# Two tile pairs by seven products beside one plain pair, in a two-block transformer kernel on one Trainium2 core

## The chip, the core and the metric

The kernel runs on one core of a Trainium2 chip. The core's engines are PE (TensorE, the matrix multiplier), DVE (VectorE), ACT (ScalarE), POOL (GpSimd) and SP (SyncE, which here issues the loads of the weights). Each runs its own instruction stream and waits for the others on semaphores. The metric is the device time of one execution in microseconds (us).

## The reference

A hidden state of 1024 features by 528 positions (16 learned ones and 512 of the input) goes through an attention layer, a gated feed-forward network (FFN), a latent-attention layer, a second FFN, and a mixing layer with a third FFN. All is float32. The change lies in the three FFNs, which compute

```
xn = rms_norm(h, g_norm)
a, b = jnp.split(xn @ w_in, 2, axis=-1)          # 2 x 2816 columns
ap = jnp.pad(a, ((0, 0), (CONV_W - 1, 0), (0, 0)))
a_conv = conv_b
for j in range(CONV_W):                          # causal, width 3
    a_conv = a_conv + ap[:, j:j + L] * conv_w[j]
return h + (jax.nn.silu(a_conv) * b) @ w_out
```

2816 columns are 22 tiles of 128, so `w_in` has 22 tile pairs: tile f of the half a, and tile 22 + f of the half b.

## The kernel before, in words

**Products.** The state lies with features on the 128 partitions (8 tiles, k = 0 to 7) and positions along the free axis. Each float32 operand is split in a high and a low part, and each product is three matmuls: high weights by high state (`Xh`), high by low (`Xl`), low by high. A weight tile of 128 outputs by 1024 features is thus 24 matmuls over some columns.

**A plain tile pair** (`plain`, L553) takes 96 matmuls of about half the columns: two pieces of tile a, two of tile b. In the second FFN tile b, and in the third both tiles, go in one piece of 512 columns (24 matmuls) in place of two of 256. Each result goes through DVE and ACT (`gate`: convolution, SiLU) to the tile `G`, input of `w_out`.

**A tile pair by seven products** (`pair`, L565) is Winograd's form of a 2 by 2 block product: the blocks are the two tiles by two halves of the features, against two halves of the features by two halves of the positions (H = 264, 258 or 256 columns). Seven block products of 12 matmuls each (84 in all) replace eight. They need sums of weight blocks and differences of state blocks. With a1 and a2 the two weight tiles of a pair, four weight sets are made in turn, and I name them by the `kind` in the plan of weights: "a" (a1 itself, products p1 and p2), "s" (a2's first half plus its second, and that less a1's first half: p5 and p6), "t" (two more differences, written over a1: p7 and p3), "d" (a2's second half: p4). The differences of the state (`T`, as `Th` and `Tl`) are made once in an FFN by `differences` (L489 to L509), behind the first plain pair. Each seven is interleaved with one plain pair, and PE keeps that order as written (`in_order`); the other engines' orders are set by a scheduler.

**Weights** (`Weights`, L79 to L173). A plan lists the weight tiles in the order of their use. Loads of 512 KB run three entries ahead on SP (L101), into a pool of three raw buffers; the second row a2 of a seven has one buffer of its own, "rawA". The split in high and low runs two entries ahead: ACT casts the high part (L147, `whi`), DVE subtracts the low part (L154, `wlo`), or POOL does (L151) for kind "d" and for plain tiles with n % 4 == 3. There are four buffers for split weights, and one more ("ws") for kind "s". POOL makes the sums (L110): those of kind "s" in one buffer "rawS", those of kind "t" over a1. The differences of the state are also made in the buffer "rawS" (L497).

**The FFN** runs its 22 tile pairs in three groups (`GROUPS`, L59). In each, `group_h` then multiplies the group's part of `G` by `w_out` (matmuls into `po`).

Of the kernel before, what the change touches and what calls it, by code (L numbers as in the profile page):

```python
# [12 lines left out]
F32 = mybir.dt.float32  # L13
# [8 lines left out]
P = 128  # L22
D = 1024
KD = D // P
META = 16
# [15 lines left out]
def _layout_params():  # L41
# [15 lines left out]
NPAR = _layout_params()  # L57

GROUPS = (  # L59
# [3 lines left out]
)  # L63

WSPEC = [
# [13 lines left out]
class Weights:  # L79
# [7 lines left out]
    def __init__(self, net, plan, gains, raw, parts, load_ahead, split_ahead):  # L87
        self.net, self.plan, self.gains = net, plan, gains
        self.raw, self.parts = raw, parts
        self.la, self.sa = load_ahead, split_ahead  # L90
        self.nl = self.ns = self.nu = 0
        self.raws, self.split = {}, {}
        self.more = None

    def load(self):
        key, aps, nk, nc_, kind = self.plan[self.nl]
        ts = []
        for i, ap in enumerate(aps):
            pool, tag, kw = (self.more, "rawA", {"bufs": 1}) if i else (self.raw, "raw", {})
            t = pool.tile([P, 1024], F32, tag=tag, name=f"raw{self.nl}_{i}", **kw)  # L100
            self.net.nc.sync.dma_start(t[:, : ap.shape[-1]], ap)  # L101
            ts.append(t)
        if ts:
            self.raws[self.nl] = ts
        self.nl += 1

    def sums(self, d, a, b, op):
# [4 lines left out]
    def source(self, n, kind, w):  # L112

        lo, hi = slice(0, 512), slice(512, 1024)
        if kind == "":
            return self.raws.pop(n)[0][:, :w]
        if kind == "a":
            self.A = self.raws.pop(n)
            return self.A[0]
        a1, a2 = self.A  # L120
        if kind == "s":
            self.S = self.more.tile([P, 1056], F32, tag="rawS", name=f"rawS{n}", bufs=1)
            self.sums(self.S[:, lo], a2[:, lo], a2[:, hi], ALU.add)
            self.sums(self.S[:, hi], self.S[:, lo], a1[:, lo], ALU.subtract)
            return self.S[:, :1024]
        if kind == "t":
            self.sums(a1[:, lo], a1[:, lo], a2[:, lo], ALU.subtract)
            self.sums(a1[:, hi], a1[:, hi], self.S[:, hi], ALU.subtract)
            return a1
        return a2[:, hi]  # L130

    def _split(self):
        nc = self.net.nc
# [53 lines left out]
class Net:  # L187
# [60 lines left out]
    def plan_ffn(self, wi, wo):  # L248
        pl = []
        for k0, k1, steps in GROUPS:  # L250
            for st in steps:
                if isinstance(st, int):
                    pl += [self.chunk(wi, st), self.chunk(wi, NF + st)]
                    continue
                f, g = st
                rows = [self.chunk(wi, m)[1][0] for m in (f, NF + f)]
                pl += [((wi, f, "a"), rows, 8, P, "a"), ((wi, f, "s"), [], 8, P, "s"), self.chunk(wi, g)]
                pl += [((wi, f, "t"), [], 8, P, "t"), self.chunk(wi, NF + g), ((wi, f, "d"), [], 4, P, "d")]
            pl += [self.chunk(wo, m, k0, k1) for m in range(KD)]
        return pl  # L260

# [206 lines left out]
    def ffn(self, wi, wo, cw, cb, a_ranges, b_ranges, quads, ranges, nxt, gain=None):  # L468
# [11 lines left out]
        with ExitStack() as cx:  # L480
# [9 lines left out]
            def differences():  # L490

                for k in range(4):
# [6 lines left out]
                    nc.vector.tensor_tensor(d[:, 0], x2, x1, op=ALU.subtract)  # L499
                    nc.vector.scalar_tensor_tensor(  # L500
                        d[:, 2], self.h[:, k + 4, s1:e1], g, x2, op0=ALU.mult, op1=ALU.subtract
                    )
                    nc.vector.tensor_tensor(d[:, 1], d[:, 2], x1, op=ALU.add)
                    nc.vector.scalar_tensor_tensor(
                        d[:, 3], self.h[:, k + 4, s0:e0], g, d[:, 1], op0=ALU.mult, op1=ALU.subtract
                    )
                    hi, lo = (t[:, :, k, :] for t in T)
                    nc.scalar.copy(hi, d)
                    nc.vector.tensor_tensor(lo, d, hi.bitcast(F32), op=ALU.subtract)  # L509

            def block(ps, w, c, x, first=True):

# [28 lines left out]
            def half_a(w, am, s, e, first=False):  # L541
                ps = bank(first)
                self.lin(ps[:, : e - s], w, X, s, e)
                nc.vector.tensor_tensor(am[:, s - a0 : e - a0], ps[:, : e - s], R[:, s:e], op=ALU.mult)

            def half_b(w, t, s, e, first=False):
                ps = bank(first)
                self.lin(ps[:, : e - s], w, X, s, e)
                nc.vector.tensor_tensor(t[:, s - t0 : e - t0], ps[:, : e - s], t[:, s - t0 : e - t0], op=ALU.mult)

            def plain(f, k):
                w = [(self.W.get((wi, f, 0)), 0)]
                am = tp.tile([P, NT], F32, tag="am", name=self.n("am"))  # L553
                for z, (s, e) in enumerate(a_ranges):
                    half_a(w, am, s, e, f == 0 and z == 0)
                t = gate(f, am)
                w = [(self.W.get((wi, NF + f, 0)), 0)]
                for z, (s, e) in enumerate(b_ranges):
                    half_b(w, t, s, e, f == 0 and z == 0)
                self.split(*G.at(k, t0, NT), t)  # L560

            def pair(f, kf, g, kg):

                get = self.W.get
                A, B, C = bank(True), None, bank()  # L565
                wa = get((wi, f, "a"))
                block(A, wa, 0, (0, 0))
                p1 = tp.tile([P, H], F32, tag="p1", name=self.n("p1"), bufs=1)
                nc.scalar.copy(p1, A[:, :H])
                ws = get((wi, f, "s"))  # L570
                block(C, ws, 0, 0)
                bm = tp.tile([P, NT], F32, tag="bm", name=self.n("bm"), bufs=1)
                sl, hi = slice(e0 - s1, H), slice(e0 - a0, NT - a0)
                nc.scalar.copy(bm[:, hi], C[:, sl])
                am = tp.tile([P, NT], F32, tag="am", name=self.n("am"))
                w = [(get((wi, g, 0)), 0)]
                half_a(w, am, *a_ranges[0])
                block(A, ws, 4, 1, False)
                u2 = tp.tile([P, H], F32, tag="u2", name=self.n("u2"), bufs=1)
                nc.scalar.copy(u2, A[:, :H])  # L580
                B = bank()
                block(B, wa, 4, (1, 0))
                an = tp.tile([P, NT], F32, tag="am", name=self.n("am"))
                nc.vector.tensor_tensor(an[:, :H], p1, B[:, :H], op=ALU.add)
                for s, e in a_ranges[1:]:
                    half_a(w, am, s, e)
                t = gate(g, am)
                wt = get((wi, f, "t"))
                block(A, wt, 0, 2, False)
                nc.vector.tensor_tensor(bm[:, hi], A[:, sl], bm[:, hi], op=ALU.add)  # L590
                w = [(get((wi, NF + g, 0)), 0)]
                half_b(w, t, *b_ranges[0])
                block(C, wt, 4, (1, 1), False)
                nc.vector.tensor_tensor(an[:, hi], u2[:, sl], C[:, sl], op=ALU.add)
                block(A, get((wi, f, "d")), 0, 3, False)
                nc.scalar.copy(bm[:, :H], A[:, :H])
                for s, e in b_ranges[1:]:
                    half_b(w, t, s, e)
                self.split(*G.at(kg, t0, NT), t)
                nc.vector.tensor_tensor(an[:, : NT - a0], an[:, : NT - a0], R[:, a0:], op=ALU.mult)  # L600
                t = gate(f, an)
                nc.vector.tensor_tensor(t, bm[:, o : o + n], t, op=ALU.mult)
                self.split(*G.at(kf, t0, NT), t)
# [4 lines left out]
            for k0, k1, steps in GROUPS:  # L608
                for i, st in enumerate(steps):
                    if isinstance(st, int):  # L610
                        plain(st, st - k0)
                    else:
                        with self.in_order():
                            pair(st[0], st[0] - k0, st[1], st[1] - k0)
# [1088 lines left out]
    def run(self):  # L1703
# [9 lines left out]
        quads = ((14, 272), (270, NT))  # L1713
        self.ffn("w_in1", "w_out1", "cw1", "cb1", ((14, 272), (272, NT)), REAL, quads, REAL, nxt, "fin_norm")
        self.mixer()
        quads = ((META, 272), (272, NT))
        self.ffn("w_up", "w_dn", "cw2", "cb2", REAL, REAL, quads, REAL, None)


def build(tc, ins, out):  # L1720
# [110 lines left out]
```

## Time and profile before

| | |
|---|---|
| median of 3 runs | 2130.53 us (2129.2 to 2133.52) |
| the profiled execution's own time | 2129.86 us |
| its span, first to last instruction | 2128.0 us |
| PE busy | 2054.2 us, 97% of the span |
| DVE, ACT, POOL busy | 63%, 44%, 28% |
| granted clock of PE, mean | 0.986 of full speed |
| matmul instructions | 13505 |
| DMA, mean | 82 GB/s |

The span is cut in instructions by engine; what is idle on PE is the part that other engines can shorten. In a row of the timeline the columns are the start, the duration, the engine and line, the operation with output and inputs, and, in brackets, the idle time before it and what ended that. Matmuls are pipelined, so the distance between two starts is what one costs, not its duration. PEclk is the granted clock as a share of full speed.

### The profile page before, as it was taken

Reading aid. Unit: us, or ns where it says so; the run is one execution under the profiler, and the core shown is the slowest. Engines: PE = TensorE matmul, PEld = TensorE weight load, DVE = VectorE, ACT = ScalarE, POOL = GpSimd, SP = SyncE. Lnnn points to the kernel's source line nnn. Section 1 sums busy time; section 2 is a strip of 40 time slices with the busy share of each in tenths; the row PEclk is TensorE's granted clock in tenths of the full one; section 3 lists DMA queues with packets and bytes.
Section 4 is the critical chain, followed back from the end, with each engine's and each line's share of the span. In section 5 each row is a group of like instructions: output and inputs, shape, how many; then the busy total and the mean of one; then the engine's idle time right before and its main releaser. Section 6 shows DMA issues by size and latency. Waiting matters only on the chain.

```text
span 2128.0 us, 34085 instructions
## 1 busy us (share of the span) xinstructions
PE 2054.2 (97%) x13505; PEld 1861.4 (87%) x13505; DVE 1335.5 (63%) x2410; ACT 935.7 (44%) x1778; POOL 600.2 (28%) x723
## 2 busy tenths in 40 slices
PE   8999997999999999997999999999999997999998
PEld 8999897999999988897989898788888886888887
DVE  8787766647387576656748378675433456647373
ACT  6666554424255455444425255344332344434243
POOL 5223232322132232032223235221022132233222
PEclk9999999999999999998999999999999998999999
DMA  4111022313223111021323223222122321322231
GB/s 167 51 60 60 31 90 70 109 62 120 87 91 102 47 40 41 31 90 41 119 80 113 86 87 117 79 90 74 61 90 89 104 99 60 101 97 92 87 103 66
DMA packets 52960, 174.78 MB, mean 82 GB/s; under 512 B 6080, under 2 KB 9024, under 8 KB 52800
## 3 DMA queue, kind: packets, MB, share of 16 engines
q1 hardware_dynamic: 52368, 172.34, 24.8%
q8 instruction: 106, 1.74, 0.3%
q14 instruction: 54, 0.44, 0.1%
q10 hardware_dynamic: 432, 0.27, 0.0%
HBM read 170.45 MB, written 2.10 MB: 81 GB/s over the span
## 4 chain that ended last, share of the span: by engine, by line
PE 79%; DVE 9%; issue 5%; ACT 4%; POOL 2%; DMA 2%; SPq 0%; ACTq 0%; POOLq 0%; DVEq 0%
PE po L302 24%; PE pf L302 16%; PE pf L522 10%; PE pc L302 6%; PE pg L302 4%; PE pq L302 3%; DVE wlo L154 2%; PE pyc L302 2%; PE s L651 2%; PE pm L302 2%; PE pd L302 2%; ACT whi L147 1%; PE ph L302 1%; PE o L1291 1%; DMA raw<-in_w_up_dram 1%
## 5 line engine op out<-in xcount | busy, mean ns | idle before, releaser
L147 ACT CAST whi<-raw 128x1024 fp32r<-128x1024 f32 (+3 forms) x355 | 346.6, 979 | 528.8 <-PE po L302 212.4
L151 POOL TENSOR_TENSOR wlo<-raw,whi 128x256 fp32r<-128x256 f32 (+1 forms) x294 | 231.0, 815 | 793.5 <-ACT whi L147 771.0
L154 DVE TENSOR_TENSOR wlo<-raw,whi 128x512 fp32r<-128x512 f32 (+2 forms) x528 | 361.1, 726 | 65.8 <-ACT whi L147 63.5
L302 PE MATMUL pf<-Xh,whi 128*128 128x264 f32 (+3 forms) x936 | 301.3, 322 | 0.0
L302 PE MATMUL pf<-Xl,whi 128*128 128x264 f32 (+3 forms) x936 | 300.7, 321 | 0.0
L302 PE MATMUL pf<-Xh,wlo 128*128 128x264 f32 (+3 forms) x936 | 300.2, 321 | 0.0
L302 PE MATMUL po<-Gl,whi 128*128 128x512 f32 (+2 forms) x711 | 240.0, 339 | 0.0
L302 PE MATMUL po<-Gh,wlo 128*128 128x512 f32 (+2 forms) x711 | 238.6, 337 | 0.0
L302 PE MATMUL po<-Gh,whi 128*128 128x512 f32 (+2 forms) x711 | 238.3, 338 | 0.0
L302 PEld LDWEIGHTS pf<-Xh,wlo 128*128 128x128 f32 x936 | 177.6, 190 | 13.3
L302 PEld LDWEIGHTS pf<-Xh,whi 128*128 128x128 f32 x936 | 177.6, 190 | 12.1
L302 PEld LDWEIGHTS pf<-Xl,whi 128*128 128x128 f32 x936 | 177.5, 190 | 11.4
L522 PE MATMUL pf<-Th,whi 128*128 128x264 f32 (+2 forms) x432 | 124.9, 289 | 41.4 <-ACT whi L147 38.2
L302 PEld LDWEIGHTS po<-Gh,wlo 128*128 128x128 f32 x711 | 133.8, 188 | 15.9
L302 PEld LDWEIGHTS po<-Gh,whi 128*128 128x128 f32 x711 | 133.0, 188 | 16.0
L302 PEld LDWEIGHTS po<-Gl,whi 128*128 128x128 f32 x711 | 133.5, 188 | 15.2
L522 PE MATMUL pf<-Th,wlo 128*128 128x264 f32 (+2 forms) x432 | 124.4, 288 | 0.1
L522 PE MATMUL pf<-Tl,whi 128*128 128x264 f32 (+2 forms) x432 | 123.8, 287 | 0.0
L522 PEld LDWEIGHTS pf<-Th,whi 128*128 128x128 f32 x432 | 83.2, 193 | 43.5 <-ACT whi L147 38.8
L302 PE MATMUL pq<-Xh,whi 128*128 128x272 f32 (+1 forms) x384 | 114.5, 298 | 1.4 <-ACT whi L147 1.4
L302 PE MATMUL pq<-Xl,whi 128*128 128x272 f32 (+1 forms) x384 | 111.3, 290 | 2.2 <-DVE Xl L403 2.2
L302 PE MATMUL pq<-Xh,wlo 128*128 128x272 f32 (+1 forms) x384 | 111.0, 289 | 0.6 <-DVE wlo L154 0.6
(423 smaller groups left out, 5219.0 us busy)
## 6 DMA issues: line engine op xcount, KB each, us to landing
raw<-in_w_in_dram SPq DMA_DIRECT2D x134, 512.0 KB, 3.5
raw<-in_w_up_dram SPq DMA_DIRECT2D x44, 512.0 KB, 3.6
raw<-in_w_out_dram SPq DMA_DIRECT2D x32, 448.0 KB, 3.4
raw<-in_w_qkv_dram SPq DMA_DIRECT2D x24, 512.0 KB, 3.5
raw<-in_w_o_dram SPq DMA_DIRECT2D x16, 512.0 KB, 3.5
raw<-in_w_out_dram SPq DMA_DIRECT2D x16, 512.0 KB, 3.9
raw<-in_w_dn_dram SPq DMA_DIRECT2D x16, 448.0 KB, 3.4
raw<-in_w_co_dram SPq DMA_DIRECT2D x8, 512.0 KB, 3.6
```

Source lines behind the costliest of these rows:

```text
L147: nc.scalar.copy(h, r)
L151: nc.gpsimd.tensor_tensor(l[:, c], r[:, c], h[:, c].bitcast(F32), op=ALU.subtract)
L154: nc.vector.tensor_tensor(l[:, c], r[:, c], h[:, c].bitcast(F32), op=ALU.subtract)
L302: nc.tensor.matmul(ps, w, x, start=first and i == 0, stop=i == len(ops) - 1, skip_group_check=not first)
L522: nc.tensor.matmul(ps[:, :H], a, b, start=first and i == 0, stop=i == len(ops) - 1, skip_group_check=not first)
L651: nc.tensor.matmul(s[:, :w], qa[:, q0 : q0 + P], ka[:, k0:k1], start=z == 0, stop=z == len(ops) - 1 and not masked,)
L1291: nc.tensor.matmul(o[:, i, j, :], st[n, "pt", j][:, b * P : (b + 1) * P], V[:, b, c], start=n % 4 == j == b == 0, stop=False,)
```

## The change

- `GROUPS`: 11 pairs go by seven products and 11 plain, where it was 9 and 13. Three plain pairs stand ahead of the first seven of an FFN, where it was two. Five of the steps in an FFN are triples: two sevens x and y by turns with one plain pair v. The sixth, (6, 7), is one seven with one plain as before.
- The order of a triple on PE is x.p1, x.p5, v.a(0), x.p6, x.p2, v.a(1), x.p7, x.p3, y.p1, x.p4, y.p5, y.p6, y.p2, v.b(0), y.p7, y.p3, v.b(1), y.p4, with v.a(0), v.a(1), v.b(0), v.b(1) the pieces of the plain pair (24 matmuls each).
- In the plan, a triple stands as a1, s1, wa, t1, a2, d1, s2, wb, t2, d2 (a, s, t, d of x with 1, of y with 2; wa and wb the plain pair's two tiles). The second row of a seven is loaded by the entry "s", where it was loaded with "a". It still has one buffer, "rawA".
- `differences` writes to buffers of its own (tags "bm" and "ct"), two casts and two subtractions a tile in place of one of each.
- In the second FFN tile b, in the third both tiles of plain pairs go in two pieces of 256 columns.

```diff
-    (0, 8, (0, 1, (2, 3), (4, 5), (6, 7))),
-    (8, 15, ((8, 9), (10, 11), (12, 13), 14)),
-    (15, 22, ((15, 16), (17, 18), (19, 20), 21)),
+    (0, 8, (0, 1, 2, (3, 4, 5), (6, 7))),
+    (8, 15, ((8, 9, 10), (11, 12, 13), 14)),
+    (15, 22, ((15, 16, 17), (18, 19, 20), 21)),
...
-            pool, tag, kw = (self.more, "rawA", {"bufs": 1}) if i else (self.raw, "raw", {})
+            pool, tag, kw = (self.more, "rawA", {"bufs": 1}) if kind == "s" else (self.raw, "raw", {})
...
+                wa, wb = self.chunk(wi, g), self.chunk(wi, NF + g)
+                if len(u) == 1:
+                    pl += [*u[0][:2], wa, u[0][2], wb, u[0][3]]
+                else:
+                    pl += [*u[0][:2], wa, u[0][2], u[1][0], u[0][3], u[1][1], wb, *u[1][2:]]
...
-                    d = tp.tile([P, 1056], F32, tag="rawS", name=self.n("d"), bufs=1)
-                    d = d[:, : 4 * H].rearrange("p (t c) -> p t c", t=4)
+                    d = [
+                        tp.tile([P, NT], F32, tag=c, name=self.n("d"), bufs=z)[:, : 2 * H]
+                        .rearrange("p (t c) -> p t c", t=2)
+                        for c, z in (("bm", 2), ("ct", 3))
+                    ]
...
+            def turns(k0, *fs):
+                u = [Seven(f, f - k0) for f in fs[:-1]]
+                v = Plain(fs[-1], fs[-1] - k0)
+                x, y = u[0], u[-1]
+                x.p1(), x.p5(), v.a(0), x.p6(), x.p2(), v.a(1), x.p7()
+                if x is y:
+                    v.b(0), x.p3(), x.p4(), v.b(1)
+                    return
+                x.p3(), y.p1(), x.p4(), y.p5(), y.p6(), y.p2(), v.b(0), y.p7(), y.p3(), v.b(1), y.p4()
...
-        self.ffn("w_in1", "w_out1", "cw1", "cb1", ((14, 272), (272, NT)), REAL, quads, REAL, nxt, "fin_norm")
+        self.ffn("w_in1", "w_out1", "cw1", "cb1", ((14, 272), (272, NT)), even, quads, REAL, nxt, "fin_norm")
...
-        self.ffn("w_up", "w_dn", "cw2", "cb2", REAL, REAL, quads, REAL, None)
+        self.ffn("w_up", "w_dn", "cw2", "cb2", even, even, even, REAL, None)
```

The first place is POOL at the second triple (11, 12, 13) of the first FFN after the change. `wlo_6168` is d1's low part, made from `raw_5934`, the second row of x; `wlo_6235` is the low part of wb; `rawS_6207` holds the s sums of y, whose second row is `raw_6172` and whose first is `raw_6058`.

```order
L149 TENSOR_TENSOR wlo_6168<-raw_5934,whi_6167 128x256 x2
L149 TENSOR_TENSOR wlo_6235<-raw_6217,whi_6234 128x256 x4
L107 TENSOR_TENSOR rawS_6207<-raw_6172 128x256 x2
L107 TENSOR_TENSOR rawS_6207<-rawS_6207,raw_6058 128x256 x2
L107 TENSOR_TENSOR raw_6058<-raw_6058,raw_6172 128x256
```

At the seven (8, 9) of before, whose next seven is (10, 11), POOL has the low part of "d" (`wlo_5747`), and right behind it the s sums (`rawS_5812`) of the next seven:

```order
L151 TENSOR_TENSOR wlo_5747<-raw_1_5430,whi_5746 128x256 x2
L110 TENSOR_TENSOR rawS_5812<-raw_1_5753 128x256 x2
L110 TENSOR_TENSOR rawS_5812<-rawS_5812,raw_0_5751 128x256 x2
L110 TENSOR_TENSOR raw_0_5751<-raw_0_5751,raw_1_5753 128x256
L110 TENSOR_TENSOR raw_0_5751<-raw_0_5751,rawS_5812 128x256
```

So the s sums of y stand behind d1's low part in the same triple, and in this triple behind four operations of a plain tile as well.

The second place is the loads on SP for the first triple of the second group, (8, 9, 10), and the start of the next, after the change. The rows are, in turn, the first row of x, wa, the first row of y, wb, the first row of the next triple's x, the second row of y (`raw_5760`), the next triple's wa, its y's first row, and its x's second row.

```order
L100 DMA raw_5437<-in_w_in_dram 128x1024
L100 DMA raw_5560<-in_w_in_dram 128x1024
L100 DMA raw_5646<-in_w_in_dram 128x1024
L100 DMA raw_5805<-in_w_in_dram 128x1024
L100 DMA raw_5901<-in_w_in_dram 128x1024
L100 DMA raw_5760<-in_w_in_dram 128x1024
L100 DMA raw_6007<-in_w_in_dram 128x1024
L100 DMA raw_6058<-in_w_in_dram 128x1024
L100 DMA raw_5934<-in_w_in_dram 128x1024
```

Before, the same stretch has the first row of (8, 9), its two plain tiles, the first row of (10, 11), its two plain tiles, and then the second row of (10, 11), `raw_1_5753`.

```order
L101 DMA raw_0_5428<-in_w_in_dram 128x1024
L101 DMA raw_0_5551<-in_w_in_dram 128x1024
L101 DMA raw_0_5637<-in_w_in_dram 128x1024
L101 DMA raw_0_5751<-in_w_in_dram 128x1024
L101 DMA raw_0_5822<-in_w_in_dram 128x1024
L101 DMA raw_0_5908<-in_w_in_dram 128x1024
L101 DMA raw_1_5753<-in_w_in_dram 128x1024
```

The second row of a seven, bound to the one buffer "rawA", is in both loaded late; after the change there are two such loads in a triple.

## Rows read from the trace of the kernel before

**Rows 1.** The cores' spans and clocks.

```profile
core 0: 2128.0 us, clock 0.986
```

**Rows 2.** Waits of PE: us in total, times, longest.

```profile
PE pf L522 <- ACT whi L147: 38.2, 3, 14.3
...
PE pf L522 <- ACT u L580: 3.2, 3, 1.9
```

**Rows 3.** Timeline of PE, first FFN, first seven.

```profile
328.28 0.28 PE L522 MATMUL pf<-Xh,wlo 128*128 128x264 f32 x1
340.01 0.59 PE L522 MATMUL pf<-Th,whi 128*128 128x264 f32 x1 [11.45 <-ACT whi L147]
...
340.86 0.59 PE L522 MATMUL pf<-Th,wlo 128*128 128x264 f32 x1
```

**Rows 4.** Windows behind gaps of PE: length, busy of engines, PEclk, DMA share, GB/s.

```profile
340.00:343.90 3.90, 3.85 (x16) 3.55 (x17) 2.20 (x3) 1.34 (x2) 2.53 (x3) 0.51 0.00 0
986.70:992.40 5.70, 5.64 (x24) 5.35 (x25) 4.00 (x6) 2.27 (x3) 2.52 (x3) 0.50 0.01 3
1775.70:1780.90 5.20, 5.15 (x17) 4.45 (x18) 3.50 (x5) 2.26 (x3) 2.52 (x3) 0.50 0.00 0
...
1941.30:1944.70 3.40, 3.40 (x15) 3.11 (x14) 3.34 (x7) 1.06 (x2) 1.50 (x2) 0.50 0.34 103
...
96.40:100.40 4.00, 4.00 (x33) 3.95 (x34) 2.16 (x7) 2.72 (x13) 0.00 (x0) 1.00 0.35 123
```

**Rows 5.** Timeline of DVE, POOL and ACT before the first gap's end.

```profile
334.39 1.25 DVE L509 TENSOR_TENSOR Tl<-d,Th 128x1056 fp32r<-128x1056 f32 x1
...
302.58 3.19 POOL L151 TENSOR_TENSOR wlo<-raw,whi 128x256 fp32r<-128x256 f32 x4 [4.62 <-ACT whi L147]
...
335.72 1.80 POOL L110 TENSOR_TENSOR rawS<-raw 128x256 f32<-128x256 f32 x2 [28.07 <-DVE Tl L509]
...
338.92 1.04 ACT L147 CAST whi<-rawS 128x1024 fp32r<-128x1024 f32 x1 [3.77 <-POOL rawS L110]
```

**Rows 6.** Timelines from one seven's p2 to the next seven's "s" weights.

```profile
461.62 0.28 PE L302 MATMUL pf<-Xh,whi 128*128 128x264 f32 x1
...
461.74 0.62 ACT L147 CAST whi<-raw 128x512 fp32r<-128x512 f32 x1 [1.00 <-PE pf L522]
464.67 1.05 ACT L147 CAST whi<-raw 128x1024 fp32r<-128x1024 f32 x1 [2.31 <-PE pf L302]
...
471.70 1.05 ACT L147 CAST whi<-rawS 128x1024 fp32r<-128x1024 f32 x1 [1.75 <-POOL rawS L110]
...
462.44 1.43 POOL L151 TENSOR_TENSOR wlo<-raw,whi 128x256 fp32r<-128x256 f32 x2 [21.91 <-ACT whi L147]
467.60 2.21 POOL L110 TENSOR_TENSOR rawS<-raw 128x256 f32<-128x256 f32 x2 [3.73 <-DMA raw<-in_w_in_dram]
...
463.89 0.33 SPq L101 DMA_DIRECT2D raw<-in_w_in_dram  x1
```

**Rows 7.** The same chain on ACT, one seven later.

```profile
484.79 0.63 ACT L147 CAST whi<-raw 128x512 fp32r<-128x512 f32 x1
...
493.85 1.05 ACT L147 CAST whi<-rawS 128x1024 fp32r<-128x1024 f32 x1 [2.47 <-POOL rawS L110]
```

**Rows 8.** Timeline of PE, distances of 264, 256 and 512 columns.

```profile
464.55 0.28 PE L522 MATMUL pf<-Th,whi 128*128 128x264 f32 x1
...
1887.08 0.28 PE L522 MATMUL pf<-Th,whi 128*128 128x256 f32 x1
...
1888.49 0.40 PE L302 MATMUL pf<-Xh,whi 128*128 128x512 f32 x1
...
1894.00 0.28 PE L522 MATMUL pf<-Th,whi 128*128 128x256 f32 x1
```

**Rows 9.** Timeline of PE, two shorter gaps.

```profile
1940.84 0.39 PE L522 MATMUL pf<-Th,whi 128*128 128x256 f32 x1 [1.85 <-ACT u L580]
...
96.38 0.39 PE L651 MATMUL s<-qk,qk 128*128 128x264 f32 x1 [2.50 <-ACT qk L818]
```

More of the change, by code (lines that the diff above doesn't have):

```diff
@@ L92, in __init__ @@
         self.raws, self.split = {}, {}
-        self.more = None
+        self.more, self.rows = None, []
     def load(self):
         key, aps, nk, nc_, kind = self.plan[self.nl]
-        ts = []
-        for i, ap in enumerate(aps):
-            pool, tag, kw = (self.more, "rawA", {"bufs": 1}) if i else (self.raw, "raw", {})
-            t = pool.tile([P, 1024], F32, tag=tag, name=f"raw{self.nl}_{i}", **kw)
+        for ap in aps:
+            pool, tag, kw = (self.more, "rawA", {"bufs": 1}) if kind == "s" else (self.raw, "raw", {})
+            t = pool.tile([P, 1024], F32, tag=tag, name=f"raw{self.nl}", **kw)
             self.net.nc.sync.dma_start(t[:, : ap.shape[-1]], ap)
-            ts.append(t)
-        if ts:
-            self.raws[self.nl] = ts
+            self.raws[self.nl] = t
         self.nl += 1
@@ L115, in source @@
         if kind == "":
-            return self.raws.pop(n)[0][:, :w]
+            return self.raws.pop(n)[:, :w]
         if kind == "a":
-            self.A = self.raws.pop(n)
-            return self.A[0]
-        a1, a2 = self.A
+            self.rows.append([self.raws.pop(n)])
+            return self.rows[-1][0]
+        a = self.rows[0]
         if kind == "s":
[L122 to L125, printed above, removed]
+            a.append(self.raws.pop(n))
+            a.append(self.more.tile([P, 1024], F32, tag="rawS", name=f"rawS{n}", bufs=1))
+            self.sums(a[2][:, lo], a[1][:, lo], a[1][:, hi], ALU.add)
+            self.sums(a[2][:, hi], a[2][:, lo], a[0][:, lo], ALU.subtract)
+            return a[2]
         if kind == "t":
[L127 to L130, printed above, removed]
+            self.sums(a[0][:, lo], a[0][:, lo], a[1][:, lo], ALU.subtract)
+            self.sums(a[0][:, hi], a[0][:, hi], a[2][:, hi], ALU.subtract)
+            return a[0]
+        return self.rows.pop(0)[1][:, hi]
     def _split(self):
@@ L254, in plan_ffn @@
                     continue
[L255 to L258, printed above, removed]
+                *fs, g = st
+                a, d = [[self.chunk(wi, m + f)[1] for f in fs] for m in (0, NF)]
+                u = [
+                    [((wi, f, "a"), a[i], 8, P, "a"), ((wi, f, "s"), d[i], 8, P, "s")]
+                    + [((wi, f, "t"), [], 8, P, "t"), ((wi, f, "d"), [], 4, P, "d")]
+                    for i, f in enumerate(fs)
+                ]
[4 more added lines that the diff above has]
+                    pl += [*u[0][:2], wa, u[0][2], u[1][0], u[0][3], u[1][1], wb, *u[1][2:]]
             pl += [self.chunk(wo, m, k0, k1) for m in range(KD)]
@@ L539, in bank @@
                 return (self.psg if first else psp).tile([P, 512], F32, tag="mm", name=self.n("pf"))
[L541 to L603, printed above, removed]
@@ new lines, in ffn, with __init__, piece, a @@
+            class Plain:
+                def __init__(me, f, k):
+                    me.f, me.k = f, k
+                    me.am = tp.tile([P, NT], F32, tag="am", name=self.n("am"))
+                def piece(me, s, e, first):
+                    ps = bank(first)
+                    self.lin(ps[:, : e - s], me.w, X, s, e)
+                    return ps[:, : e - s]
+                def a(me, i, j=1):
+                    if i == 0:
+                        me.w = [(self.W.get((wi, me.f, 0)), 0)]
+                    for s, e in a_ranges[i : i + j]:
+                        ps = me.piece(s, e, me.f == 0 and i == 0)
+                        nc.vector.tensor_tensor(me.am[:, s - a0 : e - a0], ps, R[:, s:e], op=ALU.mult)
+                    if i + j == len(a_ranges):
+                        me.t = gate(me.f, me.am)
+                def b(me, i, j=1):
+                    if i == 0:
+                        me.w = [(self.W.get((wi, NF + me.f, 0)), 0)]
+                    for s, e in b_ranges[i : i + j]:
+                        ps = me.piece(s, e, me.f == 0 and i == 0)
+                        t = me.t[:, s - t0 : e - t0]
+                        nc.vector.tensor_tensor(t, ps, t, op=ALU.mult)
+                    if i + j == len(b_ranges):
+                        self.split(*G.at(me.k, t0, NT), me.t)
@@ new lines, in ffn, with __init__, tile, p1 @@
+            class Seven:
+                lo, hi, sl = slice(0, H), slice(e0 - a0, NT - a0), slice(e0 - s1, H)
+                def __init__(me, f, k):
+                    me.f, me.k = f, k
+                def tile(me, tag, w, bufs=1):
+                    return tp.tile([P, w], F32, tag=tag, name=self.n(tag), bufs=bufs)
+                def p1(me):
+                    me.wa = self.W.get((wi, me.f, "a"))
+                    me.A = bank(True)
+                    block(me.A, me.wa, 0, (0, 0))
+                    me.u1 = me.tile("u1", H)
+                    nc.scalar.copy(me.u1, me.A[:, :H])
+                def p5(me):
+                    me.ws = self.W.get((wi, me.f, "s"))
+                    me.C = bank()
+                    block(me.C, me.ws, 0, 0)
+                    me.b = me.tile("bm", NT, 2)
+                    nc.scalar.copy(me.b[:, me.hi], me.C[:, me.sl])
+                def p6(me):
+                    block(me.A, me.ws, 4, 1, False)
+                    me.u2 = me.tile("u2", H)
+                    nc.scalar.copy(me.u2, me.A[:, :H])
+                def p2(me):
+                    B = bank()
+                    block(B, me.wa, 4, (1, 0))
+                    me.a = me.tile("am", NT, 2)
+                    nc.vector.tensor_tensor(me.a[:, :H], me.u1, B[:, :H], op=ALU.add)
+                def p7(me):
+                    me.wt = self.W.get((wi, me.f, "t"))
+                    block(me.A, me.wt, 0, 2, False)
+                    b = me.b[:, me.hi]
+                    nc.vector.tensor_tensor(b, me.A[:, me.sl], b, op=ALU.add)
+                def p3(me):
+                    block(me.C, me.wt, 4, (1, 1), False)
+                    nc.vector.tensor_tensor(me.a[:, me.hi], me.u2[:, me.sl], me.C[:, me.sl], op=ALU.add)
+                    a = me.a[:, : NT - a0]
+                    nc.vector.tensor_tensor(a, a, R[:, a0:], op=ALU.mult)
+                    me.t = gate(me.f, a)
+                def p4(me):
+                    block(me.A, self.W.get((wi, me.f, "d")), 0, 3, False)
+                    nc.scalar.copy(me.b[:, :H], me.A[:, :H])
+                    nc.vector.tensor_tensor(me.t, me.b[:, o : o + n], me.t, op=ALU.mult)
+                    self.split(*G.at(me.k, t0, NT), me.t)
@@ L610, in ffn @@
                     if isinstance(st, int):
-                        plain(st, st - k0)
+                        v = Plain(st, st - k0)
+                        v.a(0, 2), v.b(0, 2)
                     else:
                         with self.in_order():
-                            pair(st[0], st[0] - k0, st[1], st[1] - k0)
+                            turns(k0, *st)
                     if k0 == i == 0:
@@ L1712, in run @@
         nxt = functools.partial(self.open_x, gg, META)
[L1713 to L1714 removed]
+        quads, even = ((14, 272), (270, NT)), ((META, 272), (272, NT))
+        self.ffn("w_in1", "w_out1", "cw1", "cb1", ((14, 272), (272, NT)), even, quads, REAL, nxt, "fin_norm")
         self.mixer()
[L1716 to L1717 removed]
+        self.ffn("w_up", "w_dn", "cw2", "cb2", even, even, even, REAL, None)
 def build(tc, ins, out):
```

16 lines of the change are left out of this document (9 added, 7 removed).

## The prediction, made before the changed kernel ran

> **What bounds the kernel now.** I read the clock and span first, then PE's waits, then the timeline at the largest of them, then the windows behind. PE is granted 0.986 of its speed over 2128.0 us [rows 1], and the waits of PE name nearly all that others can still give back: one line, the p5 products of the sevens, waits three times for the high part of its weights, 38.2 us in all [rows 2]. The timeline shows where: the first p1 of the first seven ends at 328.28, and p5 starts at 340.01 [rows 3]. Behind each of the three gaps PE runs at about half clock, 1.2 GHz where it is 2.4 elsewhere, for 3.9, 5.7 and 5.2 us [rows 4].
>
> The cause of a gap stands in the other engines' rows. POOL idles 28.07 us, until the last subtraction of the state's differences is done (334.39 + 1.25), and then starts the sums of kind "s" [rows 5]. It doesn't need the differences: both write the one buffer "rawS". Then come two sums and the cast at 338.92, and PE goes on at its end, 339.96 [rows 3, 5].
>
> Inside the groups no such gap stands in the list of waits. The next seven's s sums are late there too, but covered. The chain is: p2 of a seven ends (461.62 is the first matmul behind it), which frees a split buffer; ACT casts "d" at 461.74; POOL makes its low part at 462.44, which is the last read of "rawA"; SP issues the load at 463.89; POOL starts the sums at 467.60; ACT casts them from 471.70 to 472.75 [rows 6]. That is 11.1 us from p2's end to the high part. One seven later it is shorter, 484.79 - 0.12 to 494.90, or 10.2 [rows 7]. The third matmul also needs the low part: behind the first gap it started 0.85 after the first [rows 3], where two distances are 0.24, so add 0.6. I take 11.3, the middle of 10.8 and 11.7.
>
> **The change part by part.** Sums are made on the profiled execution's 2129.86 us, which is 0.67 under the median of the runs.
>
> *The front.* The differences leave "rawS", so POOL can make the s sums as soon as the row is loaded. With a third plain pair ahead, PE reaches p5 96 matmuls later, 96 × 2.93 / 24 = 11.7 us (from 461.62 to 464.55 is 24 matmuls [rows 6, 8]), at 340.1. The last subtraction ended at 335.64 [rows 5]; halves of it in twice the number add little, and in the order of DVE it stands ahead of the third plain pair's last piece of a. So the gaps go: -38.2. The half clock behind them goes too: half of 14.8 us, -7.4 [rows 4]. The extra casts and subtractions (four of each in an FFN) lie beside PE's 11.7 us; without that cover each subtraction is at most 1.25 [rows 5], 5 an FFN.
>
> *Products.* A block of 12 costs 1.41 at 256 columns, and 24 of 512 cost 5.51 [rows 8], so two pieces of 256 cost 5.64, 0.13 more. First FFN: two pairs save 12 matmuls each at 0.122, -2.9. Third: two sevens (84 × 0.1175 = 9.87) in place of plains of 11.02 save 2.3, and 11 plains with two split pieces each cost 11 × 0.26 = 2.9: +0.6. Second, with one split piece, I put midway, -1.4 (with 258 columns as with 256). Sum -3.7.
>
> *The waits for the copy of p6.* 3.2 us in three, with half clock for 3.4 us behind the longest [rows 2, 4]. They come where one block stands between p6 and p7; with split pieces a quarter of the plain pair stands there too, so they go: -3.2 - 1.7 = -4.9.
>
> *The triples, stall at y.p5.* Here the cover falls. The s weights of y need the chain above, begun by x.p2: four split buffers hold a1, wa, t1 and a2, so d1's cast waits for x.p2; d1's low part frees "rawA"; then y's second row is loaded, summed, cast. Between x.p2 and y.p5 PE has v.a(1), x.p7, x.p3, y.p1 and x.p4: 24 + 4 × 12 = 72 matmuls. At the distances above that is 8.8, about 8.6 and 8.5 us in the three FFNs. Before, it was p2 to the next seven's p5, 120 matmuls, 14.6 us. So y.p5 is late by 11.3 less 8.5 to 8.8: 2.5 to 2.8, and by the two chains shown between 2.0 and 3.2. Fifteen triples by 2.67 is +40 (30 to 48). Behind y.p5 on PE everything is queued, y's products and v.b; SP's later loads are queued behind the one that waits for "rawA", but they have time.
>
> *POOL's extra.* In 8 of the 15 triples the low part of wb stands ahead of the s sums of y on POOL (as at the triple shown under the change). It can start when wb is cast, which waits for the end of v.a(1), the last to read wa: a cast of 1.05 at 464.67, 3.05 behind p2 [rows 6], so 4.1; it takes 3.19 [rows 5] and ends 7.3 behind p2. The row lands 6.0 behind it (467.60 less 461.62) [rows 6]. So +1.3 each, +10.6; nothing if wb is late or its operations run faster, so 0 to 12.
>
> *The clock.* Two shorter gaps bound it: idle 1.85 us in a stretch of thirds and copies left half clock for 3.4 us, 1.7 lost [rows 4, 9]; idle 2.50 in the attention left full clock [rows 4, 9]. No row settles which a 2.7 to 4 us stall is like. I take the first for 11 of 15, being on the same products: 11 × 1.7 = +19 (0 to 26).
> The Trainium skill, "TensorE: Matmul & The Clock Gate", section "HAM oscillation — how this bites in real kernels", tells of a loop whose every pass waits for its load and starts cold every time; here that would make all 15 pay. The gap at 1940.84 agrees with it, the one at 96.38 doesn't.
>
> *Other copies.* In the nine places where a triple is followed by another seven, the chain from y.p2 has 96 matmuls of cover, 11.3 to 11.7 us, against 10.8 to 11.7: I take 0.3 each, +3 (0 to 17, below).
>
> Sum: 2129.86 - 38.2 - 7.4 - 3.7 - 4.9 + 40 + 10.6 + 19 + 3 = 2148.3.
>
> **The rivals.**
> *A. The clock holds.* The stall is like the 2.50 us one in the attention, and the chains like the faster one, 2.2 us a stall: 15 × 2.2 = 33, with POOL's extra 10.6, no more. 2075.7 + 43.6 = 2119. The change is then faster. For it: that gap and the spread of the chains; against it: the gap at 1940.84 was shorter and cost clock. It decides where stall, extra and clock together are under 54 us over 15 triples, 3.6 each.
> *B. Every stall costs clock.* Fifteen by 1.7 is 25.5: 2148 + 6.5 = 2155. For it: all three gaps of the sevens and the copy's; against it: the attention's.
> *C. The next seven is late too.* POOL's plain low part falls in the chain behind y.p2 as well, 11.7 + 1.3 against 11.3: 1.7 to 2 in nine places, 17 in place of 3 or less: 2148 + 17 = 2165.
> *D. The chain doesn't bind.* If d1's cast doesn't wait for x.p2, the load comes some 3 us earlier and only the front counts: 2075.7 to 2085. Against it: the cast of "d" started 0.12 us behind p2 with the same four buffers [rows 6].
>
> **How the numbers follow.** Chances: forecast 0.40, A 0.28, B 0.12, C 0.10, D 0.10. A measurement here can tell about 0.2%, 4.3 us, from no change. Slower are the forecast, B and C, 0.62, less 0.02 for the forecast's low end; faster are A and D, 0.38, less 0.06 that A ends near 2130; so 0.60 slower, 0.08 same, 0.32 faster. The range from 2105 to 2166 leaves out D and the ends of A and C. The forecast's own range is 2135 to 2160.
>
> **What would show it.** After the change the waits of PE on the high part of weights should have no 11 us entry, but 15 of 2 to 4 us at the p5 of each triple's second seven, the longer ones where POOL has a plain low part ahead; POOL's first s sums in an FFN should end before the last difference; half clock should stand behind most stalls; p6's copy should be gone from the waits. The forecast is wrong if those stalls are absent or under 2 us, if the clock stays full behind them, or if a gap over 2 us remains at the front.

## The result

The changed kernel takes 2177.61 us (median of 4 runs, 2176.05 to 2179.57), the kernel before 2129.86. The ratio is 1.0224, with a 95% interval of 1.0206 to 1.0241: 48 us slower. The forecast had the sign, but 2148 and a range to 2166.

The profile after: a span of 2173.9 us, mean granted clock 0.978, and PE busy 96% of it. The waits of PE (total, times, longest) answer to [rows 2]:

```profile
PE pf L532 <- ACT whi L145: 57.4, 15, 5.0
...
PE st L370 <- POOL nr L357: 3.6, 2, 1.8
...
PE pf L532 <- DVE wlo L152: 2.6, 7, 0.8
```

Before, three waits for weights stood there with 38.2 us; now 15 with 57.4, one for each triple. The copy's 3.2 is gone. The timelines of PE at two of them, in the first and the second group of the first FFN:

```profile
360.29 0.39 PE L532 MATMUL pf<-Th,whi 128*128 128x264 f32 x1 [2.70 <-ACT whi L145]
361.13 0.39 PE L532 MATMUL pf<-Th,wlo 128*128 128x264 f32 x1 [0.34 <-DVE wlo L152]
...
505.15 0.46 PE L532 MATMUL pf<-Th,whi 128*128 128x264 f32 x1 [4.74 <-ACT whi L145]
```

Those are two kinds: by distances of starts 7 stalls have 2.4 to 3.5 us at their first matmul, and 8 have 5.0 to 5.3. The 8 are the triples in which POOL has a plain tile's low part ahead of y's s sums. The chain of the shorter kind, on ACT, POOL and SP, answers to [rows 6]:

```profile
348.79 0.62 ACT L145 CAST whi<-raw 128x512 fp32r<-128x512 f32 x1 [0.96 <-PE pf L532]
...
359.19 1.04 ACT L145 CAST whi<-rawS 128x1024 fp32r<-128x1024 f32 x1 [2.03 <-POOL rawS L107]
...
349.48 1.43 POOL L149 TENSOR_TENSOR wlo<-raw,whi 128x256 fp32r<-128x256 f32 x2 [17.89 <-ACT whi L145]
354.68 2.18 POOL L107 TENSOR_TENSOR rawS<-raw 128x256 f32<-128x256 f32 x2 [3.77 <-DMA raw<-in_w_in_dram]
356.82 2.34 POOL L107 TENSOR_TENSOR rawS<-rawS,raw 128x256 f32<-128x256 f32 x2
```

It is the chain of the prediction: d1's cast behind x.p2, its low part, 3.77 us idle for the load, two sums, the cast, and PE at the cast's end (360.23). In the longer kind, POOL's rows are:

```profile
495.67 3.76 POOL L149 TENSOR_TENSOR wlo<-raw,whi 128x256 fp32r<-128x256 f32 x4 [1.81 <-ACT whi L145]
499.39 2.34 POOL L107 TENSOR_TENSOR rawS<-raw 128x256 f32<-128x256 f32 x2
501.70 2.33 POOL L107 TENSOR_TENSOR rawS<-rawS,raw 128x256 f32<-128x256 f32 x2
```

The row of y was there when the four operations ended, and its sums stood behind them.

The clock behind the stalls, in windows of 7 us from the end of four of the 15 (length, busy of engines, PEclk, DMA share, GB/s):

```profile
360.20:367.20 7.00, 6.58 (x39) 6.37 (x40) 6.86 (x8) 4.03 (x9) 4.63 (x5) 0.76 0.07 9
505.10:512.10 7.00, 6.79 (x42) 6.49 (x43) 6.93 (x8) 3.87 (x8) 4.55 (x5) 0.76 0.08 10
1022.40:1029.40 7.00, 6.85 (x37) 6.55 (x38) 6.67 (x7) 3.33 (x7) 4.56 (x5) 0.63 0.11 11
...
1253.10:1260.10 7.00, 6.87 (x32) 6.57 (x32) 6.73 (x7) 3.75 (x8) 4.60 (x5) 0.53 0.08 11
```

Eight windows have 0.76, that is half clock for 3.4 us; the other seven 0.53 to 0.69. The lost share by 7 us, summed over the 15, is 32.4 us.

The front went as forecast. POOL's first sums, DVE's last difference, and PE's first p5's predecessor in the first FFN answer to [rows 3, 5]:

```profile
306.96 1.43 POOL L107 TENSOR_TENSOR rawS<-raw 128x256 f32<-128x256 f32 x2
308.35 1.18 POOL L357 TENSOR_TENSOR nr<-nv,mhalf 128x5 f32<-128x5 f32 x1
...
336.96 0.69 DVE L519 TENSOR_TENSOR Tl<-d,Th 128x528 fp32r<-128x528 f32 x1
...
340.02 0.28 PE L532 MATMUL pf<-Xh,whi 128*128 128x264 f32 x1
```

The s sums start 30 us before the last difference (306.96 against 336.96); PE comes to the first p1 at 340.0 and goes on without a gap. In the same rows is what the prediction did not name: a sum now stands ahead of `nr`, the power operation of the norm. In the second FFN it is two sums, and PE waits (POOL, then PE):

```profile
967.94 1.42 POOL L107 TENSOR_TENSOR rawS<-rawS,raw 128x256 f32<-128x256 f32 x2 [2.28 <-DMA raw<-in_w_in_dram]
969.31 1.18 POOL L357 TENSOR_TENSOR nr<-nv,mhalf 128x5 f32<-128x5 f32 x1
...
970.55 0.71 PE L370 MATMUL st<-ident,nr 128*128 128x128 f32 x4 [1.80 <-POOL nr L357]
```

POOL takes the sums in its order, the second waits 2.28 us for a load, and the norm behind it is late.

### The profile page after: what moved, and what is told of

It is laid out like the page before. It is cut to its first block, busy times and chain, and to the rows that moved or that the text cites. A ratio compares the mean times of both kernels' runs of the same rounds, so it can differ in the third digit from the quotient of the medians.

```text
span 2173.9 us, 36047 instructions
## 1 busy us (share of the span) xinstructions
PE 2078.4 (96%) x14369; PEld 1919.4 (88%) x14369; DVE 1394.3 (64%) x2461; ACT 954.4 (44%) x1826; POOL 706.4 (32%) x819
## 5 line engine op out<-in xcount | busy, mean ns | idle before, releaser
L145 ACT CAST whi<-raw 128x1024 fp32r<-128x1024 f32 (+4 forms) x361 | 349.0, 973 | 598.9 <-PE po L308 210.2
L149 POOL TENSOR_TENSOR wlo<-raw,whi 128x256 fp32r<-128x256 f32 (+1 forms) x342 | 279.3, 845 | 808.0 <-ACT whi L145 803.4
L308 PE MATMUL pf<-Xh,whi 128*128 128x256 f32 (+2 forms) x1056 | 297.3, 282 | 0.0
L308 PE MATMUL pf<-Xh,wlo 128*128 128x256 f32 (+2 forms) x1056 | 297.3, 282 | 0.0
L308 PE MATMUL pf<-Xl,whi 128*128 128x256 f32 (+2 forms) x1056 | 296.9, 281 | 0.0
L532 PE MATMUL pf<-Th,whi 128*128 128x264 f32 (+2 forms) x528 | 163.0, 309 | 57.4 <-ACT whi L145 57.4
L532 PE MATMUL pf<-Th,wlo 128*128 128x264 f32 (+2 forms) x528 | 162.6, 308 | 3.0 <-DVE wlo L152 2.6
L532 PEld LDWEIGHTS pf<-Th,whi 128*128 128x128 f32 x528 | 111.8, 212 | 60.6 <-ACT whi L145 60.5
L532 PE MATMUL pf<-Tl,whi 128*128 128x264 f32 (+2 forms) x528 | 160.7, 304 | 0.0
L541 DVE SCALAR_TENSOR_TENSOR ct<-am,par,ct 128x512 f32<-128x512 f32 (+4 forms) x132 | 119.2, 903 | 3.9 <-ACT ct L537 2.7
L532 PEld LDWEIGHTS pf<-Th,wlo 128*128 128x128 f32 x528 | 111.6, 211 | 6.9 <-DVE wlo L152 6.9
```

Of the source, the lines that this page charges most:

```text
L145: nc.scalar.copy(h, r)
L149: nc.gpsimd.tensor_tensor(l[:, c], r[:, c], h[:, c].bitcast(F32), op=ALU.subtract)
L308: nc.tensor.matmul(ps, w, x, start=first and i == 0, stop=i == len(ops) - 1, skip_group_check=not first)
L532: nc.tensor.matmul(ps[:, :H], a, b, start=first and i == 0, stop=i == len(ops) - 1, skip_group_check=not first)
L541: nc.vector.scalar_tensor_tensor(t[:, z:], am[:, a : a + n - z], w, t[:, z:], op0=ALU.mult, op1=ALU.add)
```

## The experiments

All are variants of the changed kernel; times are medians, and each ratio is against the kernel before, run beside it.

**Two row buffers.**

```
-            ... (self.more, "rawA", {"bufs": 1}) if kind == "s" ...
+            ... (self.more, "rawA", {"bufs": 2}) if kind == "s" ...
-        self.nrm = ... tile_pool(name="nrm", bufs=2 ...
+        self.nrm = ... tile_pool(name="nrm", bufs=1 ...
-            t = tp.tile([P, NT], F32, tag="ct", ..., bufs=3)
+            t = tp.tile([P, NT], F32, tag="ct", ..., bufs=2)
```

> The changed kernel with two buffers for a seven's second row; the 4 KB for it come from one buffer less for the convolution tile (tag ct, 2 for 3) and one for the squares (1 for 2). Theory: y.p5 waits because y's second row can be loaded only after d1's low part frees the one buffer. Then the 15 stalls (60 us) go, and the half clock behind them (about 25 us more than before): about 2092 us, 2085 to 2105. Rival, POOL itself is too slow for the sums in a triple: most of the stalls stay, 2140 to 2165. Second rival, the smaller ct pool makes new waits: over 2105 without waits at y.p5.

Measured 2085.73, ratio 0.9785 (0.9769 to 0.9802); the profiled execution has a span of 2086.8 and a clock of 0.993. No wait for weights at L532 is left in the list; of the waits in the FFNs, these lead:

```profile
PE st L370 <- POOL nr L357: 4.0, 2, 3.8
...
PE pf L532 <- ACT u L602: 1.1, 3, 0.6
```

So one buffer of 4 KB a partition is the whole difference between 48 us lost and 45 won. POOL's own speed is no bound, and two ct buffers are enough.

**The low parts of w_in's plain tiles on DVE.**

```
-            if kind == "d" or kind == "" and (n % 4 == 3 or ...
+            if kind == "d" or kind == "" and (n % 4 == 3 and key[0] not in ("w_in0", "w_in1", "w_up") or ...
```

> The changed kernel with the low parts of all plain tiles of w_in, w_up on DVE, none on POOL. Theory: the 8 stalls of 5.0 us are those with a plain tile's four operations on POOL ahead of the s sums; they fall to the 3.0 of the other seven: 16 us less, about 2162. Rival, the stall's length is set by the load or by DVE's use of the memory beside POOL: two groups of stalls stay, 2175 to 2182.

Measured 2160.29, ratio 1.0139 (1.0124 to 1.0154), 17 us less than the changed kernel. The waits of PE:

```profile
PE pf L532 <- ACT whi L145: 42.7, 15, 3.5
```

Fifteen again, but the longest 3.5 where it was 5.0: all are now of the shorter kind (3.0 to 3.8 by distances). So the four operations on POOL were the second kind's 2 us.

**The stall filled.**

```
+                    for i in range(20 if me.second else 0):
+                        nc.tensor.matmul(
+                            me.C[:, :H], me.wa[0][:, i % 4, :], X.at(i % 4, *quads[0])[0],
+                            start=True, stop=True,
+                        )
                     block(me.C, me.ws, 0, 0)
```

> The changed kernel with 20 matmuls of no use (264 columns, 2.4 us) ahead of each y.p5, in the time that PE waits there; the result is overwritten. Theory: the idle time makes the clock fall, so the half clock behind the stalls goes, while the start of y.p5 stays where it is: about 22 us less, 2150 to 2160. Rival, the clock falls for another reason (what PE does after the stall, or the stretch as a whole): no change, or some us slower, 2175 to 2190. If the extra matmuls delay y.p5 itself, as much slower as they delay it.

Measured 2168.93, ratio 1.0181 (1.0166 to 1.0197): 8.7 us less, not 22. Behind a stall that was 3 us the clock is full; behind six of the eight that were 5 us, of which some 2.4 are left, it is not. One window of each:

```profile
360.50:364.00 3.50, 3.17 (x25) 2.95 (x25) 3.46 (x4) 1.87 (x4) 2.31 (x3) 1.00 0.00 0
...
1286.20:1289.70 3.50, 3.16 (x14) 2.96 (x15) 3.47 (x4) 1.44 (x3) 2.49 (x3) 0.60 0.00 0
```

**Filled to the end** (36 such matmuls in the 8 longer stalls, 20 in the other 7; the edit is shown against the run above).

```
-                    for i in range(20 if me.second else 0):
+                    for i in range(me.fill):
```

> As the filled stall, but 36 matmuls of no use (4.4 us) in the 8 triples whose stall was 5 us; 20 in the other 7. With 20, the long stalls still had 2.6 us idle at their end and clocks of 0.58 to 1.0 behind. Theory, idle time alone makes the clock fall: now no stall leaves more than 0.7 idle, the clock stays full behind all 15, some 1 us less in each of the 8: 2158 to 2164. Rival, the extra matmuls cost as much as they save: 2166 to 2175.

Measured 2161.70, ratio 1.0146 (1.0131 to 1.0161); mean clock 0.995. A stall and its window:

```profile
497.84 4.51 PE L608 MATMUL pf<-Xh,whi 128*128 128x264 f32 x36
502.81 0.40 PE L532 MATMUL pf<-Th,whi 128*128 128x264 f32 x1 [0.45 <-ACT whi L145]
```

```profile
360.50:367.50 7.00, 6.56 (x52) 6.34 (x53) 6.85 (x8) 3.70 (x8) 4.66 (x5) 1.00 0.08 5
```

No stall of the 15 has half clock behind it here, so PE's idle time is what took the clock down, and work of no use in its place keeps it. Of the 32.4 us it gives back 15.9. The filling (8 × 36 + 7 × 20 matmuls by 0.122, 52 us) and the waits for weights still left, 14.9, are 67 where the idle time was 60, and copies are waited for by 3.1 us more: PE, at full clock, is sooner at its next wait. That is some 10 of the 16.5 that don't come back; no run shows where the rest goes.

**Pairs, three plain ahead** (8 sevens an FFN, no triples; the lines of groups 2 and 3 are as before the change).

```
-    (0, 8, (0, 1, 2, (3, 4, 5), (6, 7))),
+    (0, 8, (0, 1, 2, (3, 4), (5, 6), 7)),
...
```

> The changed kernel without triples: three plain pairs ahead, then sevens each with one plain (8 sevens and 14 plain an FFN); the difference buffers and split pieces of the change stay. Theory: the triples carry all the loss, the front all the gain: the three front gaps and their half clock go (46), the copy's wait (5); one seven fewer an FFN costs 4, split pieces 6, the late norm operation on POOL 4: about 2092, 2086 to 2098. Rival, the front gains less than 46 because the differences still come late, or the new buffers make waits: 2105 to 2130.

Measured 2093.32, ratio 0.9825 (0.9810 to 0.9839). The loss is in the triples, and the front, with all else that this run keeps of the change, is worth 38 us.

**Pairs, two plain ahead** (the grouping of before).

> The changed kernel with the grouping of before (two plain pairs ahead, 9 sevens, no triples); difference buffers and split pieces of the change stay. Theory: the s weights are early, but the last difference is done about 335.6, 971 and 1761 by the old clock of events, and PE is at p5 some 7 us sooner; so a gap of 6 to 8 with half clock stays in each FFN: 2130.9 - 3 x 4.5 - 5 + 5 = 2117, 2108 to 2124. Rival, buffers of their own are enough and the third plain pair isn't needed: 2085 to 2095.

Measured 2098.52, ratio 0.9855 (0.9837 to 0.9872): neither. The edit is only in `GROUPS`, back to its lines of before. The waits of PE at the first p5:

```profile
PE pf L532 <- ACT Th L518: 4.7, 3, 2.4
...
PE pf L532 <- DVE Tl L519: 3.2, 3, 1.3
```

A gap stays, but of 2 to 3 us and not 7: with two buffers the differences themselves are done sooner, the last at 333.5 where it was 335.6 (332.83 + 0.70 on DVE, against [rows 5]), and p5 starts on those that are ready. I had moved PE and left the differences where they were. So the buffers of their own, with two plain pairs ahead as before, give 31.5 us. With a third plain pair ahead, and one seven less an FFN, it is 37.6.

**v.b(0) ahead of y.p5.**

```
-                x.p3(), y.p1(), x.p4(), y.p5(), y.p6(), y.p2(), v.b(0), y.p7(), y.p3(), v.b(1), y.p4()
+                x.p3(), y.p1(), x.p4(), v.b(0), y.p5(), y.p6(), y.p2(), v.b(1), y.p7(), y.p3(), y.p4()
```

(and wb ahead of s2 in the plan)

> The changed kernel with the plain pair's third piece, v.b(0), moved ahead of y.p5, its fourth behind y.p2, and wb ahead of s2 in the plan; no more memory. Between x.p2 and y.p5 stand then 96 matmuls (11.5 to 11.7 us), and 96 again before the next seven's p5. The shift also takes POOL's plain tiles out from between d1's low part and the s sums. Theory, cover against a chain of 11.8 to 12.2: 15 stalls of 3.5 and 5.5 become 24 of 0.3 to 0.7, with full clock: about 2103, 2092 to 2118. Rival, a stall moves on to the next seven or to v.b(0) with its weights late: 2120 to 2160.

Measured 2140.02, ratio 1.0045 (1.0030 to 1.0060): the rival. My count was wrong: from y.p2 to the next p5 there are v.b(1), y.p7, y.p3, y.p4 and x.p1, 72 matmuls and not 96. The waits of PE:

```profile
PE pf L532 <- ACT whi L145: 16.5, 9, 3.1
PE pf L532 <- DVE wlo L152: 8.4, 23, 0.8
PE pf L532 <- DVE bm L626: 6.8, 10, 1.3
```

No y.p5 waits for its high part any more, though low parts are still waited for by up to 0.8; the nine p5 behind a triple wait for their high part, one of them 3.1. The cover of 24 matmuls went from one to the other.

**A split buffer of its own for kind d.**

```
-        pool, tag, kw = (self.more, "ws", {"bufs": 1}) if kind == "s" else (self.parts, "w", {})
+        pool, tag, kw = (self.more, "w" + kind, {"bufs": 1}) if kind and kind in "sd" else (self.parts, "w", {})
```

(512 wide for d; memory from the same two places as with two row buffers)

> The changed kernel with a split buffer of its own (512 wide) for the weights of kind d, one row buffer as in the change; the 4 KB come from the same two places as in the kernel with two row buffers. Theory: the chain is tied to x.p2 by the split buffer; with that tie cut the row is freed and loaded early, and the stalls go as with two row buffers: 2085 to 2095. Rival, the row buffer itself is what binds, so that the load is late all the same: 2120 to 2165.

Measured 2111.49, ratio 0.9910 (0.9893 to 0.9927). No p5 waits for weights, so the chain did hang on the split buffer at one end as on the row buffer at the other. But there is a new wait of PE, for DVE:

```profile
PE pf L532 <- DVE bm L626: 19.5, 6, 3.7
```

The timelines of DVE and PE in the third triple show one of the six:

```profile
493.39 1.94 DVE L152 TENSOR_TENSOR wlo<-raw,whi 128x512 fp32r<-128x512 f32 x2 [1.37 <-ACT whi L145]
495.25 0.42 DVE L626 TENSOR_TENSOR bm<-pf,bm 128x264 f32<-128x264 f32 x1
...
495.73 0.49 PE L532 MATMUL pf<-Th,whi 128*128 128x264 f32 x1 [3.19 <-DVE bm L626]
```

p4 adds to the accumulator that held p7, so it waits for the addition that reads p7's result. That addition stands on DVE behind a low part of other weights.

**Without the older taps** (leaves out two of the three terms of the convolution in each tile pair).

```
-                for d, w in ((1, w1), (2, w0)):
+                for d, w in ():
```

> The changed kernel without the two older taps of the convolution (gate's two operations on DVE in each of 66 tile pairs, some 50 us a kernel of DVE's time; the output lacks these terms). They run on DVE while POOL makes y's s sums. Theory, beside DVE's work POOL's sums take 2.2 to 2.3 us a pair where they take 1.4 alone, and that is what made the stalls longer than forecast: sums shorter by 1.3 to 1.8, so the stalls 1.3 to 1.8 shorter, and less half clock: 2178 - 15 x 1.5 - 10 = 2145, 2135 to 2155. Rival, the sums' time has nothing to do with DVE: stalls within 0.3 us of the changed kernel's, 2170 to 2180.

Measured 2160.44, ratio 1.0138 (1.0121 to 1.0155), 17 us less: the direction of the theory, half of its size. The stalls are 1.0 and 0.8 us shorter (by distances 2.0 to 2.2, and 4.2 to 4.3 but for one of 3.7, where most were 3.0 and 5.0; waits 43.5 in 15). On POOL, the two kinds:

```profile
356.13 2.18 POOL L107 TENSOR_TENSOR rawS<-raw 128x256 f32<-128x256 f32 x2 [3.72 <-DMA raw<-in_w_in_dram]
358.27 1.42 POOL L107 TENSOR_TENSOR rawS<-rawS,raw 128x256 f32<-128x256 f32 x2
...
498.53 1.42 POOL L107 TENSOR_TENSOR rawS<-raw 128x256 f32<-128x256 f32 x2
499.90 2.41 POOL L107 TENSOR_TENSOR rawS<-rawS,raw 128x256 f32<-128x256 f32 x2
```

One of the two sums fell from 2.34 to 1.42, the other kept its time, beside other operations of DVE.

**Two row buffers, the norm first.**

```
+            if self.after is not None:
+                r = self.after[:, 1:3]
+                self.net.nc.gpsimd.tensor_tensor(a[2][:, 0:512:256], r, r, op=ALU.add)
+                self.after = None
             self.sums(a[2][:, lo], a[1][:, lo], a[1][:, hi], ALU.add)
```

(`self.after` is the norm's tile `nr`, set once in an FFN by the norm; the two row buffers and the places they come from are as above.)

> The kernel with two row buffers, and in each FFN the first s sums on POOL made to wait for the norm's power operation (a two-column operation between them), so that they can't stand ahead of it. Theory: the wait of the norm's spread for that operation, 4 us in the second and third FFN of the kernel with two row buffers, goes: 2081 to 2084. Rival, the norm's other steps are late too, or p5 waits for the later sums: 2085 to 2090.

Measured 2080.64, ratio 0.9769 (0.9754 to 0.9783), the fastest of all: 97 us less than the changed kernel and 49 less than before. The waits of PE for `nr` are 1.0 us in two, in place of 4.0. Against two row buffers alone the intervals of the ratio touch each other, so the wait shows this gain better than the time.

## Why the prediction was wrong

**Right: the mechanism, and the front.** The gaps at the first sevens, their half clock and the copy's wait went (-50.5 in the sum), and the stall came at y.p5 in all 15 triples, by the chain named, in two kinds, 7 and 8. Two row buffers, and the buffer for d, show both ends of that chain.

**The step that failed is the clock's.** "I take the first for 11 of 15", +19, with full clock behind the rest: measured, all 15 lost at least 1.7, seven of them up to 3.3, 32.4 in sum. That is 13 of the 28 us between the forecast and the profiled execution after (2176.05). I had bounded it by two gaps, and set the attention's, 2.50 idle and full clock [rows 9], against the copy's, 1.85 and half clock; the bound from above, 26, took 1.7 as the most that one stall can cost, though behind the front gaps of before half clock had lasted 5.7 us [rows 4]. Nor was the attention's full clock a fixed thing. Before, both gaps of 2.50 us in the attention had it (96.38 and 208.97). In the changed kernel the same two gaps, in code that the change doesn't touch, have half clock behind them:

```profile
94.61 0.39 PE L699 MATMUL s<-qk,qk 128*128 128x264 f32 x1 [2.50 <-ACT qk L866]
```

```profile
94.60:98.60 4.00, 3.99 (x23) 3.94 (x24) 2.03 (x6) 2.20 (x10) 0.00 (x0) 0.64 0.39 125
208.80:212.80 4.00, 4.00 (x22) 3.89 (x23) 2.12 (x6) 1.35 (x6) 0.00 (x0) 0.63 0.36 123
```

So one execution's clock behind one gap couldn't bear the choice of 11 of 15. Of the rivals it was B, every stall costs clock, and B too was priced too low. The Trainium skill, "TensorE: Matmul & The Clock Gate", "HAM oscillation — how this bites in real kernels", has a loop that starts cold on every pass, and the 15 windows agree. Not every stall pays, though, as the last section shows from two variants.

**The stalls were sized too small**, 53.6 with POOL's extra and the copies, against 60.0 in the list of waits (57.4 + 2.6). Nearly all of it is in the eight longer ones: 38.3 by the waits, where the sum had 2.67 + 1.3 for each, 32. The load and the cast took what the rows of before had. The sums did not: 2.18 + 2.34 and 2.34 + 2.33 where I had 2.21 and what led to 471.70, or 4.1 for both; the plain tile's four operations took 3.76 and not the 3.19 of [rows 5], beside which DVE was busy for 1.64 us. In a triple DVE is at work beside nearly all of these operations; the run without the older taps shows that this is a cause (1.42 for 2.34), and that the taps are not the only operations of DVE that do it.

**Not named: the norm.** The s sums, made early, stand ahead of `nr` on POOL, 3.6 us. I priced the front's freed POOL work at nothing and looked only at what waited for it, not at what stood behind it on its engine. The last run shows it.

These three are 13.4 + 6.4 + 3.6 = 23 of 28 us. Of the other 4, some 2.4 lie outside the three FFNs, where the two kernels are the same: in the profiled executions the first product of the first FFN starts 1.2 us later (256.66 against 255.44), the layer behind that FFN takes 0.3 less, and the mixing layer ahead of the third FFN takes 1.5 more (366.2 against 364.7), with half clock from 1399.6 to 1403.1 where before has none. I read that as the clock of two executions and no effect of the change; it isn't shown. The rest, some 2 us, stays open.

**Rival C** (the p5 behind a triple late by 1.7 to 2) did not come: the 15 waits are all at the second sevens. **D** did not, without help: its premise, that d1's cast doesn't wait for x.p2, is what the buffer for d made true, and it gave 2111, not 2080.

## What to carry to other kernels

When work is interleaved more tightly, count for each buffer the matmuls between its release and its next use against the whole chain of refilling it; here 72 against 120 turned a hidden chain into 15 stalls, and one more buffer of 4 KB turned a loss of 48 us into a gain of 45. A stall of PE costs its length and, in the changed kernel, 1.7 to 3.3 us more at half clock. Work that is freed to run early can stand ahead of something urgent on its engine, so look there at the row behind it.

## What the runs showed of the hardware

POOL and DVE lengthen each other's operations. A pair of 128x256 sums on POOL took 1.42 us where DVE stood still (at 358.27 and 498.53 in the run without the older taps), and 2.34 beside DVE's work. One and the same operation of DVE in the changed kernel, the first with POOL idle, the second beside the sum at 356.82:

```profile
344.05 0.70 DVE L545 TENSOR_TENSOR ct<-ct,R 128x528 f32<-128x528 f32 x1
...
357.35 1.23 DVE L545 TENSOR_TENSOR ct<-ct,R 128x528 f32<-128x528 f32 x1
```

In the run without the older taps it kept 0.71 beside POOL's pair of 2.41. The next operation of DVE beside the same pair, L638, then took 1.04 (DVE and POOL, the pair's two operations by themselves):

```profile
499.88 0.71 DVE L545 TENSOR_TENSOR ct<-ct,R 128x528 f32<-128x528 f32 x1 [1.91 <-ACT ct L544]
500.69 1.04 DVE L638 TENSOR_TENSOR ct<-bm,ct 128x528 f32<-128x528 f32 x1
...
499.90 1.26 POOL L107 TENSOR_TENSOR rawS<-rawS,raw 128x256 f32<-128x256 f32 x1
501.13 1.18 POOL L107 TENSOR_TENSOR rawS<-rawS,raw 128x256 f32<-128x256 f32 x1
```

In the changed kernel, with POOL idle, L638 took 0.71:

```profile
490.16 0.71 DVE L638 TENSOR_TENSOR ct<-bm,ct 128x528 f32<-128x528 f32 x1
```

So the loss fell on both. The ends of the four operations alternate between the engines, 500.59, 501.16, 501.73 and 502.31, each some 0.6 us behind the other engine's, as if they took turns; only the first of them lost nothing.

The Trainium skill, "GPSIMD Engine Reference", "1. Specifications", says that POOL shares its interfaces to SBUF with DVE and contends with DVE's instructions of two SBUF inputs; these are such instructions, and the rows agree.

The half clock is not a function of a stall's length alone: 2.98 us by distances, at 360.29, was followed by 0.76 over 7 us, a 3.00 at 1253 by 0.53, and a 5.02 at 505.15 by 0.76. In the run with the low parts on DVE, two of the 15 stalls, both of 3.0 us (632.70 and 1158.59), have full clock behind them, and a third of 3.0, at 1017.89, has half:

```profile
632.70:636.20 3.50, 3.16 (x24) 2.95 (x25) 3.46 (x4) 1.88 (x3) 2.53 (x3) 1.00 0.00 0
...
1017.90:1021.40 3.50, 3.46 (x14) 3.16 (x15) 3.46 (x4) 1.87 (x4) 2.51 (x3) 0.50 0.00 0
```

Without the older taps, four of the seven stalls of 2.0 to 2.2 us have full clock behind them. What decides it in these cases, no run here shows.
